# MLP of an encoder layer: plain products' results added to residual rows by adding transfers, and doubled products in another order

## The chip, the cores and the metric

The kernel runs on one core of a Trainium2 chip. The metric is the time of one execution in microseconds of the device. Five engines work side by side, each with its own queue of instructions: TensorE (PE; its weight loads are PEld), VectorE (DVE), ScalarE (ACT), GpSimd (POOL) and SyncE (SP), which here only issues transfers. Each runs its instructions in order; what one waits for holds up all that stands behind it. Sixteen DMA engines carry the transfers.

## What is computed

One encoder layer on a sequence of 2048 rows of width 1024, in float32: a mixer with two kinds of attention, then an MLP with squared ReLU. The change concerns the MLP:

```python
x = x + gt1 * (mixed @ w_o[l])
h = rmsnorm(x, g_norm2[l]) * (1.0 + sc2) + sh2
x = x + gt2 * (jnp.square(jax.nn.relu(h @ w1[l])) @ w2[l])
```

`w1` is 1024 x 4096 and `w2` 4096 x 1024. `gt2` is one factor per output column; the kernel works on transposed data, so there it is one factor per partition, `mod[:, 5 * KT + row]`.

## The kernel before

Every float32 operand is split in a high and a low part, and a product is three matmuls (hi*hi, hi*lo, lo*hi). For each operand tile of 128 x 512 ScalarE makes the high part by a cast, and VectorE the low part by a subtraction (`operand`, L1306, into the pool `opp` of eight tiles).

The MLP is a list of *steps* (L1989 runs it). Each step gives TensorE 12 matmuls (6 in a doubled product). Work that goes beside it is put at a step's number by `at(n, job)` (L1334) or some steps later by `later.add(k, job)`. The order on TensorE and on SP is that of the program.

The sequence is cut in four blocks of 512 (`tb` = 2 * `mb` + `odd`) and the width in rows of 128 (`row` = 4 * `r` + `n`). Both matrix products of the MLP are done in the manner of Strassen and Winograd, with seven products of halves in place of eight. So a product's result goes into several blocks of the output. The residual rows lie in DRAM as `scr_x[tb, row]`, 128 x 512 each (L108), and are read, added to and written back until the last addition goes to `out`.

The stages, in order:

1. `Mixed`: the output projection of the mixer.
2. `First` for half 1 (`mb` = 1): 16 x 7 products `h @ w1`; results go to `scr_hid`.
3. The *plain* products 1 and 6 of half 1 (`Second`, L1590, 16 steps each): `hid @ w2`, into four banks that ScalarE copies to four tiles `Second.whole["s", n]` at the end of product 1 (in the profile `cs`), and to which VectorE adds product 6 at its end.
4. `First` for half 0, 112 steps.
5. Plain product 1 of half 0; the *doubled* product 7; plain product 6 of half 0; then the doubled products 5, 2, 3, 4. A doubled product (`Outer`, L1721, order in `DOUBLE`, L1285) multiplies both halves by another seven small products, 7 x 8 steps. Their right operands `halves[pr, g]` are four loaded tiles per kind (`half`, L1796) and sums of them (`half_sum`, L1802, VectorE, 128 x 1024, in the profile `r<-r,r`). The sums of kinds 6, 7 and 4 are needed in each doubled product; a sum of kind 5 only in doubled product 5. `plan` says at which steps they are made. At the end of a small product VectorE weighs its bank into residual tiles (`load_x`, L1784; `txo` and `cxo` in the profile), which SP then stores. Doubled products 5 and 7 have two such tiles per bank and the others one.

The plain products' results are added by `update` (L1647). For each of the four `n` it does three things at three different steps: SP loads the residual row into a tile; VectorE weighs the result into it (`weigh`, L1640: tile = result * factor + tile, one SCALAR_TENSOR_TENSOR); SP stores the tile, three steps later. There are eight such calls of four rows each, 32 rows in all:

- block (`r` 0, `odd` 1), which takes product 1 alone: within plain product 6 of each half;
- the other three blocks of half 1, which take the sum of 1 and 6: in the 56 steps from the start of `First` for half 0, with the two tiles of the pool `rp` (L89) as homes (`xu` in the profile);
- the other three blocks of half 0: one each in doubled products 2, 3 and 4 (`txu`, from the pool `tp` of seven tiles, L1298).

The last addition to a row must be the one that writes `out`; for the block (`r` 1, `odd` 0) of half 0 that is the update in doubled product 4.

Of the kernel before, what the change touches and what calls it, by code (L numbers as in the profile page):

```python
# [9 lines left out]
F32 = mybir.dt.float32  # L10
F32R = mybir.dt.float32r
BF16 = mybir.dt.bfloat16
AF = mybir.ActivationFunctionType
# [66 lines left out]
def encoder_kernel(ctx, tc, xT, c, g1, g2, w_in, w_rest, gqk, bias, w_o, w1, w2, w_ada, b_ada, out):  # L80
# [3 lines left out]
    osp = Ordered(tc, nc.sync)  # L84

    WIN, NEAR = 640, 384
    cpool = ctx.enter_context(tc.tile_pool(name="cpool", bufs=1))
    dram = ctx.enter_context(tc.tile_pool(name="dram", bufs=1, space=DRAM))
    rp = ctx.enter_context(tc.tile_pool(name="rp", bufs=2))  # L89
# [85 lines left out]
        rsqrt(y, v, t)  # L175
        return y

    def norm_diagonal(pl, y, tg):
        dg = pl.tile([P, 4, P], F32, tag="ndg", name=f"ndg{tg}", bufs=1)
        dve.tensor_tensor(  # L180
            dg, ident.unsqueeze(1).to_broadcast([P, 4, P]), y.unsqueeze(2).to_broadcast([P, 4, P]), op=ALU.mult
        )
        return dg

    def norm_rstd(pl, pp, acc, tg, meanwhile=None):
        y = norm_powers(pl, norm_columns(pp, acc, tg), tg)
        if meanwhile:
            meanwhile()
        return norm_diagonal(pl, y, tg)

    def norm_spread(pp, dg, tg):
        pr = pp.tile([P, TB], F32, tag="ps", name=f"pr{tg}")
# [485 lines left out]
    if True:  # L678
# [426 lines left out]
        def finish_row(g, n, ps, xr):  # L1105

            residual(g, n, ps, xr)
            if g < 2 and drain:
                return
            stores.pop()()  # L1110
            if g < 2:
                return

            def square():
                sq = rows[g] if n == 0 else op.tile([P, TB], F32, tag="otmp", name=f"sq{g}_{n}")
                act.activation(sq, xr, AF.Square)
                if n:
                    soon.append(lambda: add(sq))

            def add(sq):  # L1120
                pool.tensor_tensor(rows[g], rows[g], sq, op=ALU.add)
                if n == KT - 1:
                    later.add(3, second)

            def second():
                pv = norm_columns(dense, rows[g], f"m{g}")

                def powers():
                    y = norm_powers(op, pv, f"m{g}")
                    later.add(2, lambda: spread(y))  # L1130

                later.add(1, powers)

            def spread(y):
                dg = norm_diagonal(op, y, f"m{g}")
                later.add(2, lambda: third(dg))

            def third(dg):
                pr = dense.tile([P, TB], F32, tag="ps", name=f"prm{g}")
                for i in range(4):  # L1140
                    pe.matmul(pr[:, i * P : (i + 1) * P], ones, dg[:, i, :], start=True, stop=True)
                later.add(1, lambda: dve.tensor_copy(rows[g], pr))

            if n == 0:
                rows[g] = rp.tile([P, TB], F32, tag="r", name=f"r{g}")
            soon.append(square)
# [135 lines left out]
    NP = DFF // P // 2  # L1282
    HK = KT // 2
    PLAIN = (1, 6)
    DOUBLE = (7, 5, 2, 3, 4)  # L1285
    OUTER = (1, 5, 6, 3, 7, 2, 4)
    OUTER_NAME = {1: "11", 2: "12", 4: "22"}
    HOME = {1: 1, 2: 1, 5: 5, 3: 5, 6: 6, 7: 6, 4: 6}
# [7 lines left out]
    if True:  # L1296
# [43 lines left out]
        def norm2(tb, step):  # L1340

            acc = rp.tile([P, TB], F32, tag="r", name=f"r{tb}")
            xs = {}

            def load(k):
                xs[k] = temp(f"xn{tb}_{k}")
                sp.dma_start(xs[k], scr_x[tb, k])

            def add(k):
                x = xs.pop(k)  # L1350
                act.activation(x if k else acc, x, AF.Square)
                if k:
                    dve.tensor_tensor(acc, acc, x, op=ALU.add)

            def second():
                dg = norm_rstd(np2, fresh, acc, f"m{tb}")

                def third():
                    pr = bank(f"r{tb}", fresh)
                    for i in range(4):  # L1360
                        pe.matmul(pr[:, i * P : (i + 1) * P], ones, dg[:, i, :], start=True, stop=True)
                    dve.tensor_copy(acc, pr)
                    rows[tb] = acc

                later.add(6, third)

            for k in range(KT):
                at(step + 3 * k, lambda k=k: load(k))
                at(step + 3 * k + 4, lambda k=k: add(k))
            at(step + 3 * KT + 4, lambda: later.add(3, second))  # L1370
# [85 lines left out]
        class First(Step):  # L1456
# [29 lines left out]
            def fetch(self, m=None):  # L1486
                d = self.load()
                for n in range(4) if m is None else (m,):
                    pr, a, b, op = ((5, "21", "22", ALU.add), (6, 5, "11", ALU.subtract), (3, "12", 6, ALU.subtract), (7, "11", "21", ALU.subtract))[n]
                    if pr == 7:  # L1490
                        t = d["21"]
                    elif pr == 5 and not self.mb:
                        t = np2.tile([P, 4, P], F32, tag="ndg", name=f"s{self.nm}_{pr}", bufs=1).rearrange("p a b -> p (a b)")
                    else:
                        t = temp(f"s{self.nm}_{pr}")
                    d[pr] = column_sum(dve, t, d[a], d[b], op)
                return d
# [142 lines left out]
        def weigh(x, a, n):  # L1640
            dve.scalar_tensor_tensor(x, a, mod[:, 5 * KT + n : 5 * KT + n + 1], x, op0=ALU.mult, op1=ALU.add)

        def rows_of(t, mb, n, odd):
            tb = 2 * mb + odd
            return t[n * P : (n + 1) * P, tb * TB : (tb + 1) * TB]

        def update(mb, r, odd, loads, adds, home=None, last=False):  # L1647

            xs = {}

            def fetch(n):
                xs[n] = x = (home or temp)(f"xu{mb}_{r}{odd}_{n}")
                sp.dma_start(x, scr_x[2 * mb + odd, HK * r + n])

            def add(n):
                x, row = xs[n], HK * r + n
                weigh(x, Second.whole["s", n], row)
                dst = rows_of(out, mb, row, odd) if last else scr_x[2 * mb + odd, row]
                later.add(3, lambda: sp.dma_start(dst, x))

            for n in range(HK):
                at(loads[n], lambda n=n: fetch(n))
                at(adds[n], lambda n=n: add(n))

        def plain(mb, i):

            f = len(steps)
            steps.extend(Second(mb, i, j) for j in range(NP))
            if i == 6:
                spread = lambda *ns: [f + n for n in ns]  # L1670
                update(mb, 0, 1, spread(0, 1, 2, 8), spread(4, 5, 6, 12))
            return f

        def outer_sums(i, m, step):
# [46 lines left out]
        class Outer(Step):  # L1721
# [62 lines left out]
            def load_x(self, b):  # L1784
                home = kept if self.i in (5, 7) and b in ("22", "11") else temp
                for n in range(2):
                    Outer.outs[b, n] = []
                    for r, odd in {2: ((0, 1),), 3: ((0, 0),), 4: ((1, 1),), 7: ((1, 1), (1, 0)), 5: ((0, 0), (1, 0))}[self.i]:
                        mb, row = 2 - int(b[1]), HK * r + 2 * (int(b[0]) - 1) + n
                        x = home(f"xo{self.i}_{b}_{n}{odd}")  # L1790
                        sp.dma_start(x, scr_x[2 * mb + odd, row])
                        Outer.outs[b, n].append((x, mb, row, odd, self.i in (2, 3, 4) or (self.i == 5 and mb and r)))

        halves = {}

# [78 lines left out]
        for mb in (1, 0):  # L1874
# [22 lines left out]
            if mb:  # L1897
# [10 lines left out]
                    at(n - 7 - max(0, end + 4 - n) // 2, steps[n].load)  # L1908
                rest = len(steps)
                lent = lambda nm: rp.tile([P, TB], F32, tag="r", name=nm)  # L1910
                for n, (r, odd) in enumerate(((0, 0), (1, 1), (1, 0))):
                    at_row = rest + 3 + 16 * n
                    update(1, r, odd, range(at_row, at_row + 16, 4), range(at_row + 4, at_row + 20, 4), lent)
            else:
                at(begin - 8, steps[begin].load)
                at(begin - 6, steps[begin].fetch)
# [10 lines left out]
        for i in DOUBLE:  # L1927
            f = outer(i, plan)
            e = len(steps)
            if i == 7:  # L1930
                plain_loads(plain(0, 6), [12, 11, 11, 11, 9, 8])
            spread = lambda *ns: [f + n for n in ns]
            if i == 2:
                update(0, 0, 0, spread(8, 16, 24, 32), spread(14, 22, 30, 38))
                pass
            if i == 3:
                update(0, 1, 1, spread(8, 16, 24, 32), spread(14, 22, 30, 38))
            if i == 4:
                update(0, 1, 0, spread(8, 16, 24, 32), spread(14, 22, 30, 38), None, True)
            plan = {"load": {1: (f + 16, 4), 5: (f + 17, 2), 3: (f + 30, 2), 2: (f + 46, 2)}}  # L1940
            plan["sum"] = {6: (e - 4, 4), 7: (e + 12, 4), 4: (e + 28, 4)}
            if i == 7:
                plan["sum"] = {5: (e + 1, 2), 6: (e + 8, 2), 7: (e + 28, 4), 4: (e + 44, 4)}

        blocks = [right_blocks(1, k, kept if k else temp) for k in range(HK)]

# [104 lines left out]
```

## Time and profile before

| | |
|---|---|
| median of three runs | 2542.36 us (2541.83 to 2547.02) |
| the profiled execution | 2545.14 us |
| its span, first to last instruction | 2543.4 us |
| granted TensorE clock, mean | 0.999 |
| DMA queue of SP: moved, share of 16 engines | 707.43 MB, 81.2% |

The page gives, for each engine, the busy time within the span. Other views used below are: the busy time in stretches of the span, groups of instructions, waits (who waited for whom), the chain of waits (the work that ended last, followed back), and instructions in order of time. "SPq" is SP's queue of transfers; the name before the arrow is what is written and those behind it are what is read. `ps` and `ps_s` are banks of TensorE, `opr`, `ol`, `opw`, `oph` and `opv` operand tiles.

### The profile page before, as it was taken

How to read it: one execution, taken by the hardware profiler on the slowest of the kernel's cores; microseconds unless marked ns; L12 is line 12 of the kernel's file. 1: busy time of each engine (PE TensorE's matmuls, PEld its weight loads, DVE VectorE, ACT ScalarE, POOL GpSimd, SP SyncE). 2: the span in 40 equal slices, each digit the busy share in tenths (PEclk: the TensorE clock that was granted, in tenths of full speed). 3: DMA queues.
4: the chain of work that ended last, by engine and by line, in shares of the span. 5: the costliest groups of instructions: out<-in, count | busy, mean ns of one | idle time of the engine just before them, and what ended most of it. 6: DMA issues, size and time to landing. Idle time of an engine off the chain costs nothing.

```text
span 2543.4 us, 39545 instructions
## 1 busy us (share of the span) xinstructions
PE 2513.3 (99%) x12388; PEld 2095.6 (82%) x12388; DVE 2053.9 (81%) x3609; ACT 1510.3 (59%) x2893; POOL 746.0 (29%) x1128
## 2 busy tenths in 40 slices
PE   9999999999999999999999999999999999999999
PEld 7888888888888888887988888888878888888887
DVE  7656767887789878999768777779877759899998
ACT  6333425668866677666755555566545546566665
POOL 4330154777776667776620000000000000000000
PEclk9999999999999999999999999999999999999999
DMA  9879969789977788866787889995998996868884
GB/s 362 323 296 365 351 267 301 208 243 287 290 234 237 236 250 274 265 212 206 218 310 254 302 279 318 329 362 195 328 331 283 313 365 261 329 241 308 282 300 124
DMA packets 305361, 714.66 MB, mean 281 GB/s; under 512 B 32768, under 2 KB 92160, under 8 KB 293504
## 3 DMA queue, kind: packets, MB, share of 16 engines
q1 hardware_dynamic: 303856, 707.43, 81.2%
q10 hardware_dynamic: 1296, 4.72, 0.5%
q8 instruction: 98, 1.61, 0.3%
q14 instruction: 111, 0.91, 0.1%
HBM read 485.00 MB, written 227.02 MB: 280 GB/s over the span
## 4 chain that ended last, share of the span: by engine, by line
PE 80%; DVE 10%; ACT 4%; issue 3%; DMA 3%; POOL 1%; SPq 0%; DVEq 0%; POOLq 0%; ACTq 0%
PE ps L42 24%; PE ps_s L42 14%; PE pt L42 11%; PE acc L42 6%; PE wt L42 6%; PE pf L42 4%; PE z L42 4%; PE po L42 4%; PE pq L42 3%; DVE opr L42 2%; DVE p L42 2%; PE cz L42 1%; DVE ol L42 1%; PE ct L42 1%; DVE r L42 1%
## 5 line engine op out<-in xcount | busy, mean ns | idle before, releaser
L42 PE MATMUL ps<-h,opw 128*128 128x512 f32 x1512 | 358.6, 389 | 0.0
L42 ACT CAST wth<-wt 128x512 fp32r<-128x512 f32 (+3 forms) x544 | 257.0, 483 | 166.7 <-PE wt L42 157.5
L42 POOL TENSOR_TENSOR b<-p 128x512 f32<-128x512 f32 (+1 forms) x320 | 292.0, 912 | 168.7 <-DVE p L42 93.8
L42 DVE TENSOR_TENSOR wtl<-wt,wth 128x512 fp32r<-128x512 f32 (+3 forms) x544 | 291.0, 546 | 57.6 <-ACT wth L42 55.6
L42 PEld LDWEIGHTS ps<-h,opw 128*128 128x128 f32 x1512 | 283.7, 188 | 58.9
L42 PE MATMUL pt<-w,ht 128*128 128x512 f32 x1248 | 288.2, 391 | 0.0
L42 PE MATMUL ps_s<-h,opw 128*128 128x512 f32 x1152 | 279.4, 392 | 4.0 <-DVE cp L42 3.4
L42 PEld LDWEIGHTS pt<-w,ht 128*128 128x128 f32 x1248 | 233.0, 188 | 47.7
L42 DVE TENSOR_TENSOR_SCAN p<-z,p,zero 128x512 f32<-128x512 f32 x192 | 245.7, 1281 | 25.6 <-ACT z L42 18.1
L42 PEld LDWEIGHTS ps_s<-h,opw 128*128 128x128 f32 x1152 | 216.8, 189 | 51.1 <-DVE cp L42 4.7
L42 ACT CAST opr<-r 128x512 fp32r<-128x512 f32 x280 | 174.4, 624 | 134.5 <-PE ps L42 75.9
L42 PE MATMUL ps<-opr,ol 128*128 128x512 f32 x960 | 222.2, 390 | 0.7 <-DVE opr L42 0.6
L42 PE MATMUL acc<-wth,v 128*128 128x512 f32 (+3 forms) x544 | 220.6, 410 | 0.0
L42 PEld LDWEIGHTS ps<-opr,ol 128*128 128x128 f32 x960 | 179.6, 188 | 40.9 <-DVE opr L42 3.5
L42 ACT ACTIVATE z<-z 128x512 f32<-128x512 f32 (+1 forms) x320 | 166.5, 521 | 55.4 <-PE z L42 49.4
L42 DVE TENSOR_TENSOR opr<-r,opr 128x512 fp32r<-128x512 f32 x280 | 184.9, 687 | 10.7 <-ACT opr L42 9.9
L42 PE MATMUL z<-k,q 128*128 128x512 f32 (+3 forms) x640 | 185.7, 372 | 7.7 <-DVE p L42 7.0
L42 PE MATMUL acc<-wtl,v 128*128 128x512 f32 (+3 forms) x544 | 185.4, 347 | 0.0
L42 PE MATMUL ps<-oph,opv 128*128 128x512 f32 x768 | 176.0, 390 | 0.8 <-DVE oph L42 0.3
L42 PE MATMUL wt<-ident,b 128*128 128x128 f32 x1088 | 171.3, 273 | 0.9 <-DVE p L42 0.6
L42 PEld LDWEIGHTS ps<-oph,opv 128*128 128x128 f32 x768 | 143.9, 188 | 32.4 <-DVE oph L42 1.2
L42 PEld LDWEIGHTS wt<-ident,b 128*128 128x128 f32 x1088 | 136.4, 140 | 41.4 <-DVE wtl L42 1.7
(219 smaller groups left out, 4904.0 us busy)
## 6 DMA issues: line engine op xcount, KB each, us to landing
r<-scr_hid SPq DMA_DIRECT2D x80, 512.0 KB, 6.5
q<-scr_q SPq DMA_DIRECT2D x128, 256.0 KB, 5.0
w<-in_w_dram SPq DMA_DIRECT2D x64, 512.0 KB, 5.9
k<-scr_k SPq DMA_DIRECT2D x240, 128.0 KB, 4.5
v<-scr_v SPq DMA_DIRECT2D x120, 256.0 KB, 4.0
wa<-in_w_ada_dram SPq DMA_DIRECT2D x48, 512.0 KB, 6.2
ow<-scr_wo SPq DMA_DIRECT2D x24, 1024.0 KB, 5.9
l<-scr_t SPq DMA_DIRECT2D x20, 1024.0 KB, 7.3
```

What stands on the lines that cost most here:

```text
L42: return lambda *x, **y: self.tc.keep_in_program_order(f(*x, **y))
```

## The change

`update` no longer loads and stores residual rows. ScalarE scales the result by the row's factor into a tile, and POOL issues a transfer from that tile to the residual row in DRAM that adds on the way (`accum_op=ALU.add`). The blocks (1, 1) and (1, 0) share one scaled tile, so there are 24 scalings for 32 transfers. In half 1 the work comes at steps 4, 16, 28 and 40 of `First` for half 0 and the eight steps behind each; in half 0 at the same steps of doubled product 2.

The order of the doubled products becomes 7, 2, 5, 3, 4. The four sums of kind 5, which were made in plain product 6, are made in the last 14 steps of doubled product 2, and the sums of kind 6 for the product after 7 come every four steps instead of every two. Doubled product 5 now writes the block (1, 0) of both halves to `out`. The scratch for transfers issued by software grows from 256 to 1024, a pad and some small tiles move, and the norm's diagonal tile takes a tile of another name.

```diff
-    DOUBLE = (7, 5, 2, 3, 4)
+    DOUBLE = (7, 2, 5, 3, 4)
...
-        def update(mb, r, odd, loads, adds, home=None, last=False):
-
-            xs = {}
-
-            def fetch(n):
-                xs[n] = x = (home or temp)(f"xu{mb}_{r}{odd}_{n}")
-                sp.dma_start(x, scr_x[2 * mb + odd, HK * r + n])
-
-            def add(n):
-                x, row = xs[n], HK * r + n
-                weigh(x, Second.whole["s", n], row)
-                dst = rows_of(out, mb, row, odd) if last else scr_x[2 * mb + odd, row]
-                later.add(3, lambda: sp.dma_start(dst, x))
-
-            for n in range(HK):
-                at(loads[n], lambda n=n: fetch(n))
-                at(adds[n], lambda n=n: add(n))
+        def gather(mb, r, odd, n, x):
+            pool.dma_start(scr_x[2 * mb + odd, HK * r + n], x, accum_op=ALU.add)
+
+        def scaled(x, n, r):
+            row = HK * r + n
+            act.activation(x, Second.whole["s", n], AF.Identity, scale=mod[:, 5 * KT + row : 5 * KT + row + 1])
+            return x
+
+        def update(mb, n, step, home, last):
+
+            def one(r, odd):
+                x = scaled(home(f"xu{mb}_{r}{odd}_{n}"), n, r)
+                later.add(1, lambda: gather(mb, r, odd, n, x))
+
+            def two():
+                x = scaled(Second.whole["s", n], n, 1)
+                later.add(1, lambda: gather(mb, 1, 1, n, x))
+                at(step + 8, lambda: gather(mb, 1, 0, n, x))
+
+            if last:
+                at(step, lambda: one(0, 0))
+                at(step + 4, two)
+            else:
+                at(step, lambda: one(0, 1))
...
-                update(mb, 0, 1, spread(0, 1, 2, 8), spread(4, 5, 6, 12))
+                for n, step in enumerate((4, 5, 6, 12)):
+                    update(mb, n, f + step, temp, False)
...
-                        Outer.outs[b, n].append((x, mb, row, odd, self.i in (2, 3, 4) or (self.i == 5 and mb and r)))
+                        Outer.outs[b, n].append((x, mb, row, odd, self.i in (2, 3, 4) or (self.i == 5 and r > 0)))
...
-                for n, (r, odd) in enumerate(((0, 0), (1, 1), (1, 0))):
-                    at_row = rest + 3 + 16 * n
-                    update(1, r, odd, range(at_row, at_row + 16, 4), range(at_row + 4, at_row + 20, 4), lent)
+                for n in range(HK):
+                    update(1, n, rest + 4 + 12 * n, lent, True)
...
             if i == 2:
-                update(0, 0, 0, spread(8, 16, 24, 32), spread(14, 22, 30, 38))
-            if i == 3:
-                update(0, 1, 1, spread(8, 16, 24, 32), spread(14, 22, 30, 38))
-            if i == 4:
-                update(0, 1, 0, spread(8, 16, 24, 32), spread(14, 22, 30, 38), None, True)
+                for n, step in zip((2, 3, 0, 1), range(f + 4, f + 52, 12)):
+                    update(0, n, step, temp, True)
...
+            if i == 2:
+                plan["sum"] = {5: (e - 14, 3), 6: (e - 2, 4), 7: (e + 13, 4), 4: (e + 28, 4)}
             if i == 7:
-                plan["sum"] = {5: (e + 1, 2), 6: (e + 8, 2), 7: (e + 28, 4), 4: (e + 44, 4)}
+                plan["sum"] = {6: (e + 8, 4), 7: (e + 28, 4), 4: (e + 44, 4)}
...
-    nc = _bacc.Bacc("TRN2", target_bir_lowering=False, num_devices=1, dynamic_dma_scratch_size=256)
+    nc = _bacc.Bacc("TRN2", target_bir_lowering=False, num_devices=1, dynamic_dma_scratch_size=1024)
```

More of the change, by code (lines that the diff above doesn't have):

```diff
@@ L86, in encoder_kernel @@
     WIN, NEAR = 640, 384
+    padl = ctx.enter_context(tc.tile_pool(name="padl", bufs=1))
+    padl.tile([P, 40], F32, tag="pad", name="padl")
     cpool = ctx.enter_context(tc.tile_pool(name="cpool", bufs=1))
@@ L176, in norm_powers, with norm_diagonal @@
         return y
-    def norm_diagonal(pl, y, tg):
-        dg = pl.tile([P, 4, P], F32, tag="ndg", name=f"ndg{tg}", bufs=1)
+    def norm_diagonal(pl, y, tg, home=None):
+        if home is None:
+            dg = pl.tile([P, 4, P], F32, tag="ndg", name=f"ndg{tg}", bufs=1)
+        else:
+            dg = home.rearrange("p (a b) -> p a b", b=P)
         dve.tensor_tensor(
@@ L183, in norm_diagonal, with norm_rstd @@
         return dg
-    def norm_rstd(pl, pp, acc, tg, meanwhile=None):
+    def norm_rstd(pl, pp, acc, tg, meanwhile=None, home=None):
         y = norm_powers(pl, norm_columns(pp, acc, tg), tg)
@@ L188, in norm_rstd @@
             meanwhile()
-        return norm_diagonal(pl, y, tg)
+        return norm_diagonal(pl, y, tg, home)
     def norm_spread(pp, dg, tg):
@@ L1134, in spread @@
             def spread(y):
-                dg = norm_diagonal(op, y, f"m{g}")
+                dg = norm_diagonal(op, y, f"m{g}", op.tile([P, TB], F32, tag="otmp", name=f"ndgm{g}"))
                 later.add(2, lambda: third(dg))
@@ L1355, in second @@
             def second():
-                dg = norm_rstd(np2, fresh, acc, f"m{tb}")
+                dg = norm_rstd(padl, fresh, acc, f"m{tb}", None, np2.tile([P, TB], F32, tag="ndg", name=f"ndgm{tb}", bufs=1))
                 def third():
@@ L1492, in fetch @@
                     elif pr == 5 and not self.mb:
-                        t = np2.tile([P, 4, P], F32, tag="ndg", name=f"s{self.nm}_{pr}", bufs=1).rearrange("p a b -> p (a b)")
+                        t = np2.tile([P, TB], F32, tag="ndg", name=f"s{self.nm}_{pr}", bufs=1)
                     else:
@@ L1645, in rows_of @@
             return t[n * P : (n + 1) * P, tb * TB : (tb + 1) * TB]
-        def update(mb, r, odd, loads, adds, home=None, last=False):
-            xs = {}
-            def fetch(n):
-                xs[n] = x = (home or temp)(f"xu{mb}_{r}{odd}_{n}")
-                sp.dma_start(x, scr_x[2 * mb + odd, HK * r + n])
-            def add(n):
-                x, row = xs[n], HK * r + n
-                weigh(x, Second.whole["s", n], row)
-                dst = rows_of(out, mb, row, odd) if last else scr_x[2 * mb + odd, row]
-                later.add(3, lambda: sp.dma_start(dst, x))
-            for n in range(HK):
-                at(loads[n], lambda n=n: fetch(n))
-                at(adds[n], lambda n=n: add(n))
+        def gather(mb, r, odd, n, x):
[15 more added lines that the diff above has]
+                at(step + 4, two)
+            else:
+                at(step, lambda: one(0, 1))
         def plain(mb, i):
@@ L1669, in plain @@
             if i == 6:
-                spread = lambda *ns: [f + n for n in ns]
-                update(mb, 0, 1, spread(0, 1, 2, 8), spread(4, 5, 6, 12))
+                for n, step in enumerate((4, 5, 6, 12)):
+                    update(mb, n, f + step, temp, False)
             return f
@@ L1931, in encoder_kernel @@
                 plain_loads(plain(0, 6), [12, 11, 11, 11, 9, 8])
-            spread = lambda *ns: [f + n for n in ns]
             if i == 2:
-                update(0, 0, 0, spread(8, 16, 24, 32), spread(14, 22, 30, 38))
-                pass
-            if i == 3:
-                update(0, 1, 1, spread(8, 16, 24, 32), spread(14, 22, 30, 38))
-            if i == 4:
-                update(0, 1, 0, spread(8, 16, 24, 32), spread(14, 22, 30, 38), None, True)
+                for n, step in zip((2, 3, 0, 1), range(f + 4, f + 52, 12)):
+                    update(0, n, step, temp, True)
             plan = {"load": {1: (f + 16, 4), 5: (f + 17, 2), 3: (f + 30, 2), 2: (f + 46, 2)}}
             plan["sum"] = {6: (e - 4, 4), 7: (e + 12, 4), 4: (e + 28, 4)}
+            if i == 2:
+                plan["sum"] = {5: (e - 14, 3), 6: (e - 2, 4), 7: (e + 13, 4), 4: (e + 28, 4)}
             if i == 7:
-                plan["sum"] = {5: (e + 1, 2), 6: (e + 8, 2), 7: (e + 28, 4), 4: (e + 44, 4)}
+                plan["sum"] = {6: (e + 8, 4), 7: (e + 28, 4), 4: (e + 44, 4)}
         blocks = [right_blocks(1, k, kept if k else temp) for k in range(HK)]
```

## The prediction

> **What bounds the kernel now.** I read the page's head first.
>
> ```profile
> span 2543.4 us, 39545 instructions
> PE 2513.3 (99%) x12388; PEld 2095.6 (82%) x12388; DVE 2053.9 (81%) x3609; ACT 1510.3 (59%) x2893; POOL 746.0 (29%) x1128
> ```
>
> TensorE is busy for 99% of the span, so no edit that leaves the matmuls alone can gain more than what TensorE still loses. The chain of waits gives the pace at which it loses nothing, and the busy times by stretch show where it falls short. I cut the stretches at the first matmul of each stage: the two plain products of half 1, the first products of half 0, then the doubled products 5, 2, 3, 4. The columns are PE, PEld, DVE, ACT, POOL, each as busy time with its count, then clock, DMA share and GB/s.
>
> ```profile
> 2506.43 10.88 PE ps_s L42 x48
> ```
>
> ```profile
> 1666.90:1755.70 88.80, 88.21 (x386) 71.92 (x385) 79.32 (x130) 64.31 (x113) 0.00 (x0) 1.00 0.77 287
> 1755.70:2066.10 310.40, 307.02 (x1345) 253.16 (x1344) 241.26 (x399) 162.06 (x288) 0.00 (x0) 0.99 0.90 307
> ...
> 2230.10:2309.10 79.00, 78.16 (x338) 62.75 (x338) 75.25 (x115) 50.41 (x86) 0.00 (x0) 1.00 0.72 256
> 2309.10:2386.40 77.30, 76.90 (x337) 62.76 (x336) 77.30 (x117) 50.44 (x86) 0.00 (x0) 1.00 0.85 305
> 2386.40:2462.70 76.30, 76.30 (x337) 63.00 (x337) 75.10 (x113) 50.46 (x86) 0.00 (x0) 1.00 0.83 289
> 2462.70:2539.20 76.50, 76.48 (x337) 62.82 (x336) 71.22 (x107) 46.93 (x80) 0.00 (x0) 1.00 0.48 152
> ```
>
> 10.88/48 = 0.2267 us per matmul. The plain stage has 2 x 16 x 12 = 384 matmuls by the code (a row counts one or two that cross its edges), so it needs 87.0 and loses **1.8**. The first products have 1344, need 304.6, and lose **5.8**. A doubled product has 336 and needs 76.2: losses of 2.8, 1.1, 0.1 and 0.3, **4.3** together. That is 11.9 us in the stages that the change touches. The end stays: after the last matmul come one weighing and one transfer out, in both kernels.
>
> Most of the 5.8 lies in one place.
>
> ```profile
> 1875.00:1900.00 25.00, 22.08 (x91) 17.84 (x90) 21.24 (x35) 10.37 (x19) 0.00 (x0) 0.93 1.00 331
> ```
>
> 25 us hold 110 matmuls at full pace; here are 91, so 19 x 0.2267 = 4.3 us are missing: a gap of 25 - 22.08 = 2.9, and a clock of 0.93 around it. The chain of waits says what came before.
>
> ```profile
> 1874.04 4.86 DMA to<-scr_hid
> ...
> 1889.56 4.57 PE ps_s L42 x12
> ```
>
> TensorE waited for VectorE, which had been late since a load of `to`. VectorE and SP in order of time, with idle time and what ended it in brackets:
>
> ```profile
> 1874.47 0.69 DVE L42 TENSOR_TENSOR ts<-s,w 128x512 f32<-128x512 f32 x1 [3.82 <-DMA scr_hid<-to]
> ...
> 1879.00 1.29 DVE L42 TENSOR_TENSOR to<-cp,to 128x512 f32<-128x512 f32 x2 [0.64 <-DMA to<-scr_hid]
> ...
> 1880.81 0.75 DVE L42 SCALAR_TENSOR_TENSOR xu<-cs,mod,xu 128x512 f32<-128x512 f32 x1
> ```
>
> ```profile
> 1869.05 0.37 SPq L42 DMA_DIRECT2D scr_t<-wt  x1
> 1873.19 0.32 SPq L42 DMA_DIRECT2D xu<-scr_x  x1
> 1873.57 0.90 SPq L42 DMA_DIRECT2D to<-scr_hid  x2
> ```
>
> SP issues nothing from 1869.42 to 1873.19: the residual load `xu` wants one of two `rp` tiles, and the store of its predecessor hasn't landed. The `to` loads stand behind it. That is the rule in this stretch, not an accident (waits of SP between 1756 and 1900; then sizes and landings):
>
> ```profile
> SPq L42 <- DMA scr_x<-xu: 24.1, 10, 4.8
> ```
>
> ```profile
> xu<-scr_x SPq DMA_DIRECT2D x12, 256.0 KB, 4.4
> scr_x<-xu SPq DMA_DIRECT2D x12, 256.0 KB, 7.1
> ```
>
> **The change part by part.** It removes 32 loads and 32 stores of 256 KB from SP and 32 weighings from VectorE. It adds 24 scalings on ScalarE and 32 adding transfers on POOL's queue. And it moves half sums.
>
> *Plain stage of half 1* (4 of the 32). VectorE is full here, and a weighing stands straight in front of an operand that TensorE waits for.
>
> ```profile
> 1736.73 0.74 DVE L42 SCALAR_TENSOR_TENSOR txu<-cs,mod,txu 128x512 f32<-128x512 f32 x1
> 1737.39 0.68 DVE L42 TENSOR_TENSOR oph<-hw,oph 128x512 fp32r<-128x512 f32 x1
> ```
>
> ```profile
> 1749.95 5.90 PE L42 MATMUL ps<-oph,opv 128*128 128x512 f32 x23 [0.26 <-DVE oph L42]
> ```
>
> A weighing holds VectorE for 1737.39 - 1736.73 = 0.67. Three lie ahead of that operand, 2.0 us, more than the 1.8 lost. But ScalarE gets three scalings in the same chain:
>
> ```profile
> 1716.67 2.94 ACT L42 ACTIVATE ty<-ty,mod,aff 128x512 f32<-128x512 f32 x4
> ```
>
> 2.94/4 = 0.74 each, and ScalarE works 64 of 88.8 us here, alternating with VectorE. Bounds: 0 if they hit that alternation, -1.8 if they fall into ScalarE's pauses. I take **-1.0**.
>
> *First products of half 0* (12). SP's 24.1 us of blocking go. The `to` loads can issue up to 3.8 us sooner, which removes the 0.64 wait and, with the weighing at 1880.81 (0.67), 1.3 us of the 2.9 that VectorE was late. The 3.82 wait is another matter: it is for the landing of a store of `to`, whose own operand comes from VectorE, and nothing of the change touches it. So a gap of about 1.6 may stay; whether the clock still dips after it I can't read anywhere. Without the dip 4.3 - 1.6 = 2.7 come back. Bounds 0 (the store's landing alone sets the gap) and -5.8; I take **-3.0**, a little over 2.7, because one transfer per row takes the place of two at a DMA share of 0.90. On ScalarE 8 x 0.74 = 6 us join 162 busy ones of 310: hidden, at most 0.7 where one meets a copy that frees a bank.
>
> The adding transfer is in no row. Nearest are one store (7.1 us to landing) and load plus store (11.5). The two `rp` tiles are written every 12 steps of 2.72, so a tile comes round after 65 us, and readers of a row come 19 steps or more later, at least 25 us. Either price is covered; above 25 us SP would wait again. POOL has no other work here (0.00 in the rows), so a wait in its queue delays only the next transfer.
>
> *Doubled products.* VectorE's pace, start to start:
>
> ```profile
> 2481.13 1.22 DVE L42 TENSOR_TENSOR r<-r,r 128x1024 f32<-128x1024 f32 x1
> 2482.26 1.29 DVE L42 TENSOR_TENSOR opr<-r,opr 128x512 fp32r<-128x512 f32 x2
> 2483.47 0.68 DVE L42 TENSOR_TENSOR ol<-l,ol 128x512 fp32r<-128x512 f32 x1
> 2484.07 0.74 DVE L42 SCALAR_TENSOR_TENSOR txu<-cs,mod,txu 128x512 f32<-128x512 f32 x1
> 2484.74 0.69 DVE L42 TENSOR_TENSOR opr<-r,opr 128x512 fp32r<-128x512 f32 x1
> ```
>
> A half sum is 1.13, an operand 0.605, a weighing 0.67. Eight steps are 48 matmuls, 10.88 us, with 12 operands (7.26), usually two half sums (2.26) and two weighings (1.34): 10.86, level. A residual update makes it 11.53; product 5 with four weighings 12.20. So VectorE lives on the lead that eight operand tiles allow.
>
> Before, per product: 5 has 84 operands, 9 half sums and 24 weighings = 77.1; 2 and 3 have 12, and 12 + 4, = 75.1 each; 4 has 11 and 16 = 74.0. Sum 301.3 against 304.8.
> After: 2 follows the plain product with full lead, has 15 half sums (four of kind 5 and two of kind 6 move out of the plain product) and 12 weighings = 75.8, its last 16 steps 2.2 over TensorE's. 5 has 12 and 24 = 80.5. Then 3: 12 and 12 = 72.4; 4: 11 and 12 = 71.3. Sum 300.0.
>
> The saving is only 1.3 us of VectorE, and it comes late. Product 5 starts with some 2 us less lead, gets 1.4 of it back in eight steps with a pause in the weighings, and then meets the three blocks of 12.2 as before: it loses 2.8 + 0.8. Products 2, 3 and 4 lose no more than 0.3 of 1.5, the updates being gone. Net 3.9 for 4.3: I take **-0.5**. Bounds: +2.2 (2.8 + 2.2 + 1.5 = 6.5: none of the missing lead comes back and nothing is gained behind it) and -1.5. ScalarE takes 8 x 0.74 = 6 us in product 2 beside 50 of 77: hidden by its idle quarter.
>
> *At nothing:* the pads, the larger scratch and the new home of the norm's diagonal add no instruction. The diagonal borrows one of two tiles that POOL's adds use; cost if both are held, one such add, about 1.3 us, twice. The plain product of half 0 has slack on VectorE, which hides its four scalings' chain.
>
> Sum: -1.0 - 3.0 - 0.5 = **-4.5**. The profiled execution took 2545.14, which gives 2540.6; that is 2.8 above the median, 2542.36, from which the same sum gives **2537.9 us**.
>
> **The unknown price, and the rivals.** What does POOL's issue cost VectorE? The trace has one hint, before the MLP, beside a POOL operation on SBUF (first the tile's minimum, median and maximum in ns):
>
> ```profile
> L42 DVE TENSOR_TENSOR ndgm<-ident,nym x4: 692/976/1364, 1066.1 to 1579.3; 128x512 f32<-128x512 f32 x4
> ```
>
> ```profile
> 1212.38 2.63 POOL L42 TENSOR_TENSOR e<-e,cols 128x640 f32<-128x640 f32 x2
> ...
> 1214.19 1.36 DVE L42 TENSOR_TENSOR ndgm<-ident,nym 128x512 f32<-128x512 f32 x1
> ```
>
> A VectorE operation with both inputs in SBUF took 1364 ns beside POOL's and 692 alone: 0.67 more. Nearly all of VectorE's MLP work is of that kind.
>
> *Rival A, slower: the issue holds the shared port.* Twelve transfers start in product 2, where VectorE has no slack left. At 0.67 each that is 8.0: 2537.9 + 8.0 = 2545.9, no change. At two operations each it is 16.1: **2554**. It cancels the gain from 4.5/12 = 0.38 us each and makes the kernel measurably slower from (4.5 + 5.1)/12 = 0.8. For it: the row above. Against: POOL there reads data, a transfer's issue need not. I take none of it into the sum, and keep 0 to 16 for the range.
> The Trainium skill, page "SBUF — State Buffer", section "Who interferes with whom", says that `tensor_tensor` shares only the read interface with GpSimd, while building descriptors needs the write interface, which it calls inferred. By that rule Rival A costs nothing. The row agrees with its first half (a reading POOL operation contends, 692 to 1364); no trace of before shows the second.
>
> *Rival B: the stall stays.* The 3.82 wait is what makes VectorE late, and SP's block was beside it. Only 1.5 of the sum is left: 2540.9. For it: the store wait came first; against: VectorE's later 0.64 and 0.67.
>
> *Rival C: the whole stall goes,* with the plain stage's 1.8 and 1.5 of the doubled products: -4.3 - 1.8 - 1.5 = -7.6, **2534.8**. For it: 24 us of SP blocking vanish, and every landing in that stretch is sooner.
>
> *Rival D: transfers land late,* over 25 us, and loads wait on SP as they do now: the change doesn't do what it says, and gives back the 3.0: 2540.9 as in B.
>
> **How the numbers follow.** About 0.2%, 5.1 us, is what a measurement of this kernel can tell from no change: faster is below 2537.3, slower above 2547.4. Forecast 0.40, spread over 2535 to 2540.5, half of it on each side of 2537.3. C 0.18. B and D 0.16. A 0.26, of which 0.04 stay within 0.2%. Faster 0.20 + 0.18 = 0.38; same 0.20 + 0.16 + 0.04 = 0.40; slower 0.22. The range leaves out the far end of C below 2533 and A's upper third above 2552.
>
> **What would show it.** Right: no SP wait for `xu`; the stretch from 1875 with 100 or more matmuls; product 5 at 79 to 80 us and third in order; 3 and 4 at 76.2. Wrong: VectorE's `opr` or `ol` above 690 ns in product 2 (A); a gap of 2 us or more between steps 40 and 55 of the first products (B); SP waiting for an adding transfer (D); a new wait of ScalarE's scalings for a tile, with casts behind it.

## The result, and the profile after

The changed kernel takes **2540.05 us** (median of 19 runs, 2537.88 to 2540.97) against 2545.18 for the kernel before on the same chips (19 runs): ratio **0.9979**, 95% interval 0.9973 to 0.9986, or -5.1 us. The forecast was -4.5 us. It was set on a median of 2542.36 from three runs; over 19 runs that median is 2.8 us higher. So the 2.15 us between 2537.9 and 2540.05 come from the starting point; the change itself gained a little more than was forecast.

The head of the page after, then two of its transfer queues (packets, MB, share of 16 engines):

```profile
span 2538.1 us, 39542 instructions
PE 2510.6 (99%) x12388; PEld 2097.4 (83%) x12388; DVE 2034.1 (80%) x3577; ACT 1524.6 (60%) x2917; POOL 773.9 (30%) x1160
```

```profile
q1 hardware_dynamic: 294640, 690.65, 79.7%
q0 software_dynamic: 4608, 8.39, 2.0%
```

VectorE has 32 instructions fewer, ScalarE 24 more, POOL 32 more; SP's queue moves 16.8 MB less, and a new queue carries 8.4 MB. The busy times by stretch, cut at the first matmul of each stage as before: plain products of half 1, first products of half 0, doubled products 2, 5, 3, 4.

```profile
1668.60:1756.10 87.50, 87.39 (x386) 72.05 (x385) 77.40 (x127) 66.83 (x118) 3.66 (x4) 1.00 0.80 277
1756.10:2061.30 305.20, 304.93 (x1346) 252.31 (x1345) 232.82 (x386) 167.18 (x296) 10.40 (x12) 1.00 0.92 302
2225.30:2301.50 76.20, 76.20 (x338) 63.15 (x337) 74.23 (x111) 54.62 (x94) 10.39 (x12) 1.00 0.91 275
2301.50:2381.00 79.50, 78.31 (x337) 62.59 (x336) 79.50 (x119) 50.41 (x86) 0.00 (x0) 1.00 0.83 290
2381.00:2457.30 76.30, 76.30 (x337) 62.95 (x337) 75.02 (x113) 50.46 (x86) 0.00 (x0) 1.00 0.82 281
2457.30:2533.80 76.50, 76.44 (x338) 63.01 (x336) 69.40 (x104) 46.93 (x80) 0.00 (x0) 1.00 0.38 124
```

| stage, us | needed | before | after | moved | forecast |
|---|---|---|---|---|---|
| up to the first products of half 1 | | 1357.3 | 1359.9 | +2.6 | 0 |
| first products of half 1 | | 309.6 | 308.7 | -0.9 | 0 |
| plain products of half 1 | 87.0 | 88.8 | 87.5 | -1.3 | -1.0 |
| first products of half 0 | 304.6 | 310.4 | 305.2 | -5.2 | -3.0 |
| plain 1, doubled 7, plain 6 of half 0 | | 164.0 | 164.0 | 0 | 0 |
| the four doubled products | 304.8 | 309.1 | 308.5 | -0.6 | -0.5 |

So most of the gain lies in the first products of half 0. The 25 us that held 91 matmuls there hold 112 now, at full clock:

```profile
1875.00:1900.00 25.00, 25.00 (x112) 20.69 (x112) 21.48 (x36) 12.96 (x23) 1.74 (x2) 1.00 1.02 330
```

SP in the stretch in which it had stood still for 3.8 us, and VectorE at the `ts` that had waited 3.82:

```profile
1865.38 1.40 SPq L42 DMA_DIRECT2D to<-scr_hid  x2
1867.70 0.32 SPq L42 DMA_DIRECT2D scr_hid<-to  x1
1868.39 0.99 SPq L42 DMA_DIRECT2D to<-scr_hid  x2
```

```profile
1870.09 0.69 DVE L42 TENSOR_TENSOR opw<-w,opw 128x512 fp32r<-128x512 f32 x1 [2.52 <-ACT opw L42]
1870.70 0.68 DVE L42 TENSOR_TENSOR ts<-s,w 128x512 f32<-128x512 f32 x1
```

The four `to` loads went out at 1865.4 and 1868.4; before, their counterparts went at 1873.6 and 1875.0. VectorE no longer waits for any transfer here, only for ScalarE, and is in time. The 2.6 us before the MLP are looked at in the first experiment.

### The profile page after: what moved, and what is told of

Read it like the earlier page. It is cut to its first block, busy times and chain, and to the rows that moved or that the text cites. A ratio compares the mean times of both kernels' runs of the same rounds, so it can differ in the third digit from the quotient of the medians.

```text
span 2538.1 us, 39542 instructions
## 1 busy us (share of the span) xinstructions
PE 2510.6 (99%) x12388; PEld 2097.4 (83%) x12388; DVE 2034.1 (80%) x3577; ACT 1524.6 (60%) x2917; POOL 773.9 (30%) x1160
## 4 chain that ended last, share of the span: by engine, by line
PE 84%; DVE 7%; ACT 3%; issue 2%; DMA 2%; POOL 1%; SPq 0%; DVEq 0%; ACTq 0%; POOLq 0%
PE ps L42 26%; PE ps_s L42 15%; PE pt L42 11%; PE acc L42 6%; PE wt L42 6%; PE pf L42 4%; PE z L42 4%; PE po L42 4%; PE pq L42 3%; DVE p L42 2%; PE pso L42 2%; PE cz L42 1%; DVE opr L42 1%; PE ct L42 1%; ACT z L42 1%
## 5 line engine op out<-in xcount | busy, mean ns | idle before, releaser
L42 POOL DMA_DIRECT2D scr_x<-txu x12 | 10.5, 878 | 546.9 <-ACT txu L42 545.0
```

What stands on the lines that cost most here:

```text
L42: return lambda *x, **y: self.tc.keep_in_program_order(f(*x, **y))
```

## The experiments

My theory after the result: the gain is made by taking the residual loads off SP's queue (first products of half 0) and weighings off VectorE (plain stage), and the new order is a price. Rivals: the layout, the order, the bytes, or half 0. Differences are against the median of before, which was between 2544.2 and 2545.3 in the comparisons. Stage times are those of one profiled execution per kernel.

**1. The layout alone.** The kernel before with the pads, the norm's diagonal in another tile, and:

```diff
-dynamic_dma_scratch_size=256
+dynamic_dma_scratch_size=1024
```

> The kernel before with only the pads, the larger scratch and the norm diagonal's new home; no adding transfer. My theory (the gain is made in the MLP, by taking the residual loads off SP's queue and the weighings off VectorE, and the 2.6 us that the changed kernel's profile lost before the MLP are chance): within 1.5 us of before, and the first MLP matmul less than 1 us from its place before. Rival (the new layout costs those 2.6 us): +2.6 us, all of it before the MLP.

2546.29 us, ratio 0.9996 (0.9987 to 1.0005): no change. Its profile starts the first products of half 1 at 1359.2, 1.9 us after before's, so by one profile the start is further off than the expected 1 us. But the next two kernels have before's code and layout up to the MLP and start them at 1360.4 and 1358.1, and the nine kernels with the new layout and something of the change start them between 1357.4 and 1360.1. The 2.6 us lie inside this spread. In the changed kernel's profile 1.3 of them are TensorE's wait for a load of the output projection's weights, which the kernel before doesn't show there (waits of TensorE, 1290 to 1320):

```profile
PE po L42 <- DMA ow<-scr_wo: 1.3, 1, 1.3
```

**2. SP's queue unblocked, with nothing else.** The kernel before with half 1's updates further apart:

```diff
-                    at_row = rest + 3 + 16 * n
-                    update(1, r, odd, range(at_row, at_row + 16, 4), range(at_row + 4, at_row + 20, 4), lent)
+                    at_row = rest + 3 + 20 * n
+                    update(1, r, odd, range(at_row, at_row + 20, 5), range(at_row + 4, at_row + 24, 5), lent)
```

> The kernel before with the twelve residual updates of half 1 every five steps instead of every four, so that a residual tile's store has landed when the tile is wanted again; loads, weighings and stores all stay. My theory (SP's queue blocked behind the residual load makes the stall): SP's 24.1 us of waits for scr_x<-xu nearly gone, the 2.9 us gap gone, -3.5 to -5 us. Rival (VectorE's weighings and the bytes moved make the stall): 0 to -1 us, the gap stays.

2542.20 us, -3.0 us, ratio 0.9988 (0.9979 to 0.9997). First products of half 0, then SP's longest waits there:

```profile
1759.10:2064.40 305.30, 304.95 (x1345) 252.12 (x1344) 240.90 (x399) 162.32 (x288) 0.00 (x0) 1.00 0.91 313
```

```profile
SPq L42 <- DVE ca L42: 22.3, 6, 6.3
SPq L42 <- DVE wt L42: 10.9, 9, 4.1
```

The wait for `scr_x<-xu` is gone and the stage runs at 305.3, as in the changed kernel, although all twelve loads, weighings and stores are still there (VectorE 240.90 us, 399 instructions, as before). One step in the spacing does what the adding transfers do to this stage. The whole came out a little under the expected -3.5. In this kernel's profile the MLP starts 3.1 us later than in before's, which is the upper end of the spread of the first experiment.

**3. The order alone.** The kernel before with

```diff
-    DOUBLE = (7, 5, 2, 3, 4)
+    DOUBLE = (7, 2, 5, 3, 4)
...
+            if i == 2:
+                plan["sum"] = {5: (e - 14, 3), 6: (e - 2, 4), 7: (e + 13, 4), 4: (e + 28, 4)}
...
-                plan["sum"] = {5: (e + 1, 2), 6: (e + 8, 2), 7: (e + 28, 4), 4: (e + 44, 4)}
+                plan["sum"] = {6: (e + 8, 4), 7: (e + 28, 4), 4: (e + 44, 4)}
```

> The kernel before with only the order 7, 2, 5, 3, 4 and the half sums moved with it; updates as before. My theory (the order is a price, paid out of the weighings that the adding transfers take away): VectorE has 78.5 us of work in product 2 and 80.5 in product 5 against 76.2 of TensorE, so product 5 starts with less lead: +1 to +4 us, product 5 above 80 us. Rival (the order itself brings gain): -1 us or lower.

2546.70 us, +1.5 us, ratio 1.0006 (0.9997 to 1.0015): by the times alone not told from zero. The stages tell it (2, 5, 3, 4):

```profile
2228.70:2306.10 77.40, 77.08 (x338) 62.79 (x337) 75.42 (x113) 50.44 (x86) 0.00 (x0) 1.00 0.71 248
2306.10:2386.90 80.80, 79.08 (x337) 62.40 (x336) 80.80 (x122) 50.41 (x86) 0.00 (x0) 1.00 0.82 288
2386.90:2464.30 77.40, 77.02 (x338) 62.80 (x337) 77.40 (x117) 50.47 (x86) 0.00 (x0) 1.00 0.88 302
2464.30:2540.70 76.40, 76.40 (x337) 62.81 (x335) 71.12 (x107) 46.93 (x80) 0.00 (x0) 1.00 0.47 152
```

312.0 against 309.1: by these profiles the order costs 3 us, 1.8 of it in product 5 (80.8 against 79.0) and 1.1 in product 3 (77.4 against 76.3). In both VectorE is busy for the whole product.

**4. Half 1 alone.** New layout; adding transfers within plain product 6 and the first products of half 0 only; half 0 and the order as before. `update_by_rows` is the `update` of the kernel before.

```diff
+                if mb:
+                    for n, step in enumerate((4, 5, 6, 12)):
+                        update(mb, n, f + step, temp, False)
+                else:
+                    update_by_rows(mb, 0, 1, spread(0, 1, 2, 8), spread(4, 5, 6, 12))
```

> Adding transfers for half 1 alone (plain product 6 and the first products of half 0), with the new layout; half 0's updates and the order of the doubled products as before. My theory: the whole gain of the changed kernel is here, -5.5 to -7 us, first products of half 0 at 305 to 306 us and the doubled products at 309. Rival (gain spread over both halves, or made by the order): -1 to -3 us.

2539.88 us, -5.4 us, ratio 0.9978 (0.9969 to 0.9988): all of the gain, though just short of the expected -5.5. The plain stage and the first products:

```profile
1667.20:1754.90 87.70, 87.58 (x385) 71.98 (x384) 77.38 (x127) 66.73 (x117) 3.66 (x4) 1.00 0.80 279
1754.90:2060.30 305.40, 305.10 (x1346) 252.16 (x1345) 232.93 (x386) 167.41 (x296) 10.43 (x12) 1.00 0.92 302
```

The doubled products stay at 309.0, as expected.

**5. Half 0 alone.** The mirror image: the changed kernel with half 1 by loads, weighings and stores.

```diff
-                for n in range(HK):
-                    update(1, n, rest + 4 + 12 * n, lent, True)
+                for n, (r, odd) in enumerate(((0, 0), (1, 1), (1, 0))):
+                    at_row = rest + 3 + 16 * n
+                    update_by_rows(1, r, odd, range(at_row, at_row + 16, 4), range(at_row + 4, at_row + 20, 4), lent)
```

> The changed kernel with half 1's residual updates as before (loads, weighings, stores); adding transfers and new order for half 0 only. My theory: the stall behind SP's blocked queue stays, first products of half 0 at 308 to 312 us and the plain stage of half 1 at 88.8; the doubled products 308.5: 0 to -1.5 us against before. Rival (half 0's part brings a good share): -2.5 us or lower.

2544.81 us, -0.4 us, ratio 0.9999 (0.9989 to 1.0009): no change that can be told from zero, within the expected 0 to -1.5. The plain stage is back at 88.8 and SP's wait at 22.2 us:

```profile
SPq L42 <- DMA scr_x<-xu: 22.2, 10, 4.4
```

The first products take 306.7 in this profile, below the expected 308. With SP blocked the stage took 310.4, 312.1, 308.4 and 306.7 in four kernels, without the block 305.2 to 305.9 in the eight kernels that don't scale on VectorE. So with the block the stage varies from profile to profile, 309.4 on average against 305.5 without it, and the 5.2 us of the first comparison are 3.9 by these averages.

**6. The adding transfers in the old order.** The changed kernel with `DOUBLE` and its half sums as before; block (1, 0) of half 0 is added to the output, which product 5 has written by then.

```diff
+            dst = scr_x[2 * mb + odd, HK * r + n] if mb or odd or not r else rows_of(out, mb, HK + n, odd)
+            pool.dma_start(dst, x, accum_op=ALU.add)
```

> The changed kernel with the order 7, 5, 2, 3, 4 and its half sums as before; the adding transfers of half 0 start in product 2 as in the changed kernel, and those for block (1, 0) add to the output itself, which product 5 has written by then. My theory (by stages: the order alone cost 3.0 us, and the weighings that went gave 3.5 back): products 5, 2, 3, 4 at 78.9, 76.5, 76.3, 76.4 = 308.1 us, so within 1 us of the changed kernel, -5 to -6 us against before. Rival (the new order is needed for the gain): 309 us or more in these four, -4 us or less.

2538.51 us, -6.7 us, ratio 0.9975 (0.9965 to 0.9985). Products 5, 2, 3, 4 take 78.9, 76.4, 76.2 and 76.3: 307.8 against 308.5 in the new order. The whole is 1.5 us below the changed kernel, a little outside the expected 1 us, and the intervals of the two ratios overlap. So the new order isn't needed; that it costs 0.7 is shown by the two profiles alone.

**7. Who scales.** The changed kernel with the scalings on VectorE:

```diff
-            act.activation(x, Second.whole["s", n], AF.Identity, scale=mod[:, 5 * KT + row : 5 * KT + row + 1])
+            dve.tensor_scalar(x, Second.whole["s", n], mod[:, 5 * KT + row : 5 * KT + row + 1], 0.0, op0=ALU.mult, op1=ALU.add)
```

> The changed kernel with the 24 scalings on VectorE (tensor_scalar) instead of ScalarE; the transfers as in the changed kernel. My theory (the plain stage and the doubled products are bound by VectorE's instructions, the first products of half 0 by SP's order): eight scalings of 0.35 to 0.67 us come into product 2, so products 2 and 5 together lose 2 to 5 us more than in the changed kernel; the plain stage of half 1 between 87.5 and 88.8; first products of half 0 stay at 305 to 306. +2 to +5 us against the changed kernel. Rival (only the transfers matter, not who scales): within 1 us of the changed kernel.

2543.68 us: +3.6 us against the changed kernel, as expected; the ratio to before is 0.9993 (0.9984 to 1.0002), not told from zero. VectorE's scaling takes 480 ns where ScalarE's takes 720, and still product 2 goes from 76.2 to 77.1, product 5 from 79.5 to 80.8, the plain stage to 88.3, and the first products of half 0 to 306.6, just outside the expected 306. That the work left VectorE is a part of the gain, not only that it left SP.

**8. More adding transfers.** Twelve more in product 2, to rows that nothing reads:

```diff
+                if not mb:
+                    at(step + 8, lambda: [pool.dma_start(scr_e[n, m], Second.whole["s", n], accum_op=ALU.add) for m in range(3)])
```

> The changed kernel with twelve more adding transfers in product 2, from the same scaled tiles to rows in DRAM that nothing reads; the output is the same. My theory (a transfer's issue on POOL takes nothing from VectorE, and its bytes find room at a DMA share of 0.9): product 2 at 76.2 to 76.6 us, VectorE's operands at 686 to 690 ns, 0 to +1 us against the changed kernel. Rival A of the prediction (0.67 us of VectorE per issue): +8 us against the changed kernel, in products 2 and 5.

2546.68 us, +6.6 us against the changed kernel. The time misses the expected 0 to +1, and Rival A, near in its number, is wrong in its cause: VectorE isn't slowed. Its operands in product 2 of this run, beside 24 issues (mean 684 ns; Rival A's sign was above 690); then, in the changed kernel itself, POOL's issues beside VectorE's operations in product 2:

```profile
L42 DVE TENSOR_TENSOR opr<-r,opr 128x512 fp32r<-128x512 f32 x53 | 35.1, 684 | 2.4 <-ACT opr L42 2.4
```

```profile
2270.29 0.68 DVE L42 TENSOR_TENSOR opr<-r,opr 128x512 fp32r<-128x512 f32 x1
2270.89 0.68 DVE L42 TENSOR_TENSOR ol<-l,ol 128x512 fp32r<-128x512 f32 x1
2271.18 1.74 POOL L42 DMA_DIRECT2D scr_x<-cs  x2 [4.57 <-ACT cs L42]
2271.49 1.22 DVE L42 TENSOR_TENSOR r<-r,r 128x1024 f32<-128x1024 f32 x1
2272.62 1.28 DVE L42 TENSOR_TENSOR opr<-r,opr 128x512 fp32r<-128x512 f32 x2
```

1.22 and 0.68 beside an issue, as without one. Of the loss 5.1 us are in product 2, which takes 81.3, and 1.4 in product 5, which follows it with 80.9. The waits of product 2 name a transfer (product 2; then the longest wait of ScalarE for one; then the chain):

```profile
2225.90:2307.20 81.30, 78.33 (x337) 64.05 (x336) 73.09 (x108) 54.27 (x94) 20.78 (x24) 0.98 0.95 271
```

```profile
ACT ol L42 <- DMA l<-in_w_dram: 6.9, 1, 6.9
```

```profile
2276.30 17.11 DMA l<-in_w_dram
```

A left operand of 1 MB took 17 us to load. The queues in product 2 say why, first in the changed kernel, then here:

```profile
q1 hardware_dynamic: 7698, 17.73, 65.6%
q0 software_dynamic: 1728, 3.15, 25.1%
```

```profile
q1 hardware_dynamic: 7364, 16.18, 53.8%
q0 software_dynamic: 3168, 5.77, 41.2%
```

Twelve adding transfers keep 16 engines busy for 25.1% of 76.2 us, 19.1 us, **1.6 us each**; SP's queue moves 17.73 MB in 65.6%, 50.0 us, or 0.74 us for 256 KB. So an adding transfer costs the DMA engines about what a load and a store cost together. My reading is that product 2, at a share of 0.91 in the changed kernel, had no room for twelve more.

**9. The same number, without adding.** `accum_op` is left out of the extra twelve, which become plain copies.

> The run with twelve more transfers in product 2 once more, but these twelve are plain copies from the same tiles on POOL's queue to the same rows that nothing reads, without adding. That run lost 5.2 us in product 2 on a left operand whose load took 17 us, with the adding queue at 41.3% of the 16 engines. Theory now (an adding transfer takes the DMA engines about 1.6 us, two plain ones of 256 KB; product 2 has no room for twelve more): twelve plain ones take about 0.75 each, product 2 between 76.2 and 78, 0 to +2.5 us against the changed kernel. Rival (the number of transfers on POOL's queue, or their issue, makes the loss): +5 us or more, as with the adding ones.

2539.56 us, -0.5 against the changed kernel; product 2 takes 76.1. POOL's queue in it:

```profile
q0 software_dynamic: 2688, 6.29, 35.7%
```

The extra twelve take (0.357 - 0.251) x 76.1 / 12 = 0.67 us each. So neither the number of transfers nor POOL's issues made the loss of the run before; the adding did. That it did so by the engines' time fits the two prices, and was the theory formed after that run. The margin is thin: product 2 has a DMA share of 0.94 here without loss, and 0.95 with the loss there.

**10. A faster version.** What is left in the changed kernel is product 5, bound by VectorE. Its twelve additions to block (0, 0) go the same way:

```diff
+                        if x is None:
+                            x = temp(f"xg{self.i}_{pr}_{b}_{n}")
+                            act.activation(x, ps, AF.Identity, scale=mod[:, 5 * KT + row : 5 * KT + row + 1])
+                            later.add(1, lambda x=x, tb=2 * mb + odd, row=row: pool.dma_start(scr_x[tb, row], x, accum_op=ALU.add))
+                            continue
...
```

> The changed kernel with product 5's twelve additions to block (0, 0) made in the same manner: ScalarE scales the bank into a tile and POOL issues an adding transfer; twelve weighings, eight loads and eight stores go. My theory (product 5 is bound by VectorE, 80.5 us of work): its work falls by 12 x 0.67 = 8.0 to 72.5, product 5 goes from 79.6 to 76.3 to 76.8, -3 us against the changed kernel, -8 us against before. Rival (product 5 is late for loads, or for ScalarE, which gets 8.7 us more beside 50): product 5 stays above 78.5, within 1 us of the changed kernel.

**2536.02 us**, -9.2 us against before, ratio 0.9963 (0.9950 to 0.9977), -4.0 against the changed kernel, where -3 was expected. Products 2, 5 and 3:

```profile
2225.70:2301.80 76.10, 76.10 (x337) 63.04 (x336) 74.12 (x110) 54.62 (x94) 10.39 (x12) 1.00 0.90 276
2301.80:2378.00 76.20, 76.20 (x338) 63.06 (x337) 74.84 (x112) 56.67 (x97) 8.75 (x10) 1.00 0.92 292
2378.00:2454.20 76.20, 76.20 (x338) 63.10 (x337) 73.22 (x109) 51.11 (x88) 1.74 (x2) 1.00 0.83 279
```

Every doubled product runs at TensorE's pace. And in the old order:

> Product 5's additions to block (0, 0) by ScalarE and adding transfers, as in the fastest run so far, but in the old order 7, 5, 2, 3, 4. My theory (the order matters only through VectorE's work, and with twelve weighings gone no product of either order has more than TensorE's 76.2 us): all four doubled products at 76.1 to 76.4 us, within 1 us of that run, -8 to -10 us against before. Rival (the old order puts transfers and loads of product 5 in each other's way, or needs product 5 late): a product above 77 us, -7 us or less.

2536.39 us, -7.8, just short of the expected -8, ratio 0.9966 (0.9952 to 0.9979); products 5, 2, 3, 4 at 76.2, 76.1, 76.2 and 76.3. With VectorE below TensorE's time the order makes no difference that can be measured.

## Why the prediction was right, point by point

**The bound.** That TensorE's losses stand for all that could be gained, 11.9 us in these stages, held: the fastest version leaves about 1 of them (87.4, 305.3 and 304.8 us where 87.0, 304.6 and 304.8 are needed).

**Plain stage, -1.0:** measured -1.3. The weighings in the operands' chain were the cause: with half 1 by rows the stage is at 88.8, with the scalings on VectorE at 88.3, with them on ScalarE at 87.4 to 87.7. The fear that ScalarE's scalings would hit the alternation cost little.

**First products of half 0, -3.0:** SP's block was the cause, as forecast, but the size was too small: -5.2 by the two profiles, -3.9 by the averages. The step that failed is "nothing of the change touches it", said of the 3.82 us wait for the landing of a `to` store. VectorE writes that store's data, but SP issues it, and SP was late there already: an earlier residual load had held it from 1853.3 to 1858.4.

```profile
1852.83 0.43 SPq L42 DMA_DIRECT2D scr_x<-xu  x1
1858.40 0.32 SPq L42 DMA_DIRECT2D xu<-scr_x  x1
```

The view of the tile has the two `to` stores of this place, the second of which `ts` waits for, and their time to landing: in the kernel before, in the changed kernel, and with the other spacing, there with VectorE's `ts`.

```profile
L42 SPq DMA_DIRECT2D scr_hid<-to x2: 319/485/651, 1864.7 to 1865.7; - x2
DMA to landing us min/median/max: 8.6/8.9/9.1
```

```profile
L42 SPq DMA_DIRECT2D scr_hid<-to x2: 447/465/483, 1861.1 to 1861.7; - x2
DMA to landing us min/median/max: 7.2/7.3/7.4
```

```profile
L42 SPq DMA_DIRECT2D scr_hid<-to x2: 390/392/395, 1865.1 to 1865.6; - x2
DMA to landing us min/median/max: 8.5/8.6/8.6
1874.33 0.69 DVE L42 TENSOR_TENSOR ts<-s,w 128x512 f32<-128x512 f32 x1 [0.46 <-DMA scr_hid<-to]
```

Counted from the start of the stage, the second store goes out at 110.0, 105.6 and 106.5 us. With the other spacing it takes as long to land as before, 8.6 us, but goes out 3.5 us sooner, and the wait shrinks from 3.82 to 0.46. So the link is the time at which SP issues the store, behind its own block, and Rival B had it the wrong way round. In the changed kernel the store goes out 4.4 us sooner, lands 7.4 us after its issue, and the wait is gone. The four kernels with the block all have this wait (3.8, 5.0, 3.9 and 2.5 us), the longest with the 312.1 us and the shortest with the 306.7. The clock's dip went with the gap. The reason for taking a little over 2.7 fell too: one adding transfer in place of two transfers doesn't relieve the DMA engines, since it costs them about as much as both.

**Doubled products, -0.5:** -0.6, and the parts hold as well. For product 5 the text had 76.2 + 3.6 = 79.8, measured 79.5; products 3 and 4 at 76.3 and 76.5. The order alone gave +3 us, in products 5 and 3, where VectorE was busy throughout; the weighings that went gave it back.

**At nothing:** the layout cost nothing that could be measured. A scaling takes 0.72 us where 0.74 was taken. An adding transfer lands after 4.1 to 9.3 us, within the 25 us of cover, so Rival D didn't come about.

**Rival A** fell: VectorE's operations keep their time beside POOL's issues. The section "Who interferes with whom" of the Trainium skill's page "SBUF — State Buffer", quoted in the prediction, had inferred so, and this trace agrees (684 ns beside 24 issues). The slower side came by another way, not foreseen: doubled, these transfers fill the DMA engines, and the kernel is 6.6 us slower than the changed one.

**Rival C,** -7.6, is near what these stages did in the two profiles, -7.1, and further from the -5.8 by the averages; the 1.5 that it was to bring in the doubled products didn't come.

**The sum:** -4.5 against -5.1 (interval -3.6 to -6.9). By the averages the named stages gave -1.3 - 3.9 - 0.6 = -5.8, which is 1.3 more than was forecast; the 0.7 left to -5.1 lies within the interval and the spread of the starts ahead of the MLP. That the total came within 0.6 is in part luck: the profile from which the forecast took its 310.4 us was 1 us slower than the average with the block, which hid a part of what the failed step left out.

## What to carry to other kernels

Read the waits of the transfer queue like those of an engine: a load whose tile isn't free holds up every load behind it, and one step more between the uses can be worth as much as a new mechanism. Where an engine is level with TensorE, count its work per stage in instructions, and move whole instructions to the engine with idle time. Before a transfer is made to do arithmetic, look at the DMA share of the stage where it will run.

## What the runs showed of the hardware that was not expected

- An adding transfer of 256 KB from SBUF to DRAM takes the 16 DMA engines 1.6 us, a plain one of the same size 0.67 to 0.74; in landing time the two hardly differ (6.9 to 8.0 us medians against 7.1 for the old stores).
- Its issue takes POOL 0.86 to 0.88 us (medians by tile, single ones up to 1.2) and slows VectorE by nothing that the trace shows.
- POOL's queue isn't tied to the steps: the second transfer of a shared tile, placed three steps behind the first, went out in the same 1.74 us, since POOL had nothing to wait for.
- One VectorE operation on two SBUF tiles took 1364 ns beside POOL's arithmetic (692 at the least); others of that kind kept their usual time beside POOL's issues. Why the two differ no run here shows.
